# Modulation chunks issued as one run of eight products, and spread out over layer 0's feed-forward

## The chip, the cores and the metric

The kernel runs on one core of a Trainium2 chip. The metric is device microseconds (us) of one execution, the median of several runs.

## The reference

A transformer of two blocks on 256 tokens of width 1024, all in float32, inside tolerances that ask for nearly float32 products. The part that matters here is the first block: two layers, each with a modulation of six vectors for the tokens and six for a 256-token context, which are a small product with a large weight matrix.

```python
def adaln(cond, w_ada, b_ada):
    m = jax.nn.silu(cond) @ w_ada + b_ada
    return jnp.split(m, 6, axis=-1)
...
def first_block(x, c, ctx, c_ctx, w_ada, b_ada, g_mix, g_ffn, w_in, ...):
    for l in range(DEPTH):                      # DEPTH = 2
        sh1, sc1, gt1, sh2, sc2, gt2 = adaln(c, w_ada[l], b_ada[l])
        csh1, csc1, cgt1, csh2, csc2, cgt2 = adaln(c_ctx, w_ada[l], b_ada[l])
        h = rms_norm(x, g_mix[l]) * (1 + sc1) + sh1
        ...                                     # two attentions and a Fourier mix -> o
        x = x + gt1 * (o @ w_out[l])
        x = x + gt2 * swiglu(rms_norm(x, g_ffn[l]) * (1 + sc2) + sh2, w_gate[l], w_up[l], w_down[l])
        ...                                     # the context likewise, in layer 0 only
    return rms_norm(x, g_final)
```

`w_ada[l]` is 1024 x 6144 float32. The second block (two further layers with other attentions) has no modulation.

## The kernel before

Ordinary weights go in float32 through `raw` tiles of 128 x 2048 (1 MB). There are three of them (`raw_bufs`), filled in turn by loads that SyncE's queue issues in program order (L203). ScalarE casts each part of 1024 columns to its high half `whi` (L210), VectorE makes the low half `wlo` (L211), five of each exist, and every product of activations and weights is three matmuls: `mm3` at L336, L337 and L338. A load for a `raw` tile starts only when the tile's last reader is done.

The modulation of a layer is cut into twelve chunks (l, c) of 512 columns. `ada_chunk` (L469) takes two `raw` tiles from the same three, loads them (L483), and multiplies them without a cast: `ada_half` (L489) issues four products per tile, each with a stationary operand of 32 columns into its own 32 rows of one PSUM bank, so a chunk is eight products over two loads. The profile counts a float32 product of this kind twice, so a chunk shows as x16. `ada_columns` then copies the bank to `rows` on ScalarE (L496), transposes it in four pieces on TensorE (L498) and sums it on VectorE (L501, L502) into `mod`.

Layer 0's first four chunks have tiles of their own (`raw0`) and a fixed order. The other twenty go through `ada_chunk`: two a layer in the mixer (`ada_mid`), four a layer around the two groups of the first out-projection (`ada_att`, `out_first`), two in layer 1's `ada_gap` after the second part of the out-projection and the call that starts the feed-forward's norm (`norm_row`, `modulate`), and six, for the rest of layer 0 and the first of layer 1, in layer 0's feed-forward, at the groups that the table `ada_ffn` names (a group is two gate and two up columns with weights `w_gu`, 96 matmuls of 512 columns).

The program's order is not the engines' order. A scheduler with a model of the machine picks, for each engine, the ready instruction of best priority; `tc.cur_priority` moves work in that list, and the table `rank` holds the shifts. `together` (L316) gives its instructions a strong priority and ties the first of them to a list of instructions, here without a semaphore: the scheduler places it only once its model has those done. Each engine then runs its list strictly in that order.

Of the kernel before, what the change touches and what calls it, by code (L numbers as in the profile page):

```python
# [18 lines left out]
P = 128  # L19
# [3 lines left out]
RAW = 2048  # L23
# [232 lines left out]
class Build:  # L256
# [12 lines left out]
    ada_mid = ((0, 4), (0, 5)), ((1, 4), (1, 5))  # L269
    ada_att = ((0, 6), 0, (0, 7), (0, 9), 1, (0, 8)), ((1, 6), (1, 7), 0, 1, (1, 9), (1, 8))  # L270
    ada_gap = (), ((1, 10), (1, 11))
    ada_ffn = {3: ((0, 11), (0, 10)), 4: ((1, 0),), 8: ((1, 1),), 10: ((1, 3), (1, 2))}, {}

    rank = {"weights": 100, "weigh": -200, "qk": -200, "rope": -300, "hd2": -300, "together": 3000}

    def __init__(self, ctx, tc, d, out):
        self.tc, self.nc, self.d, self.out = tc, tc.nc, d, out
# [190 lines left out]

    def ada_chunk(self, l, c, tag="mm"):  # L469

        raws = self.ada_load(l, c, self.wp, "raw", self.raw_bufs)
        ps = self.bank(tag)
        for i in range(2):
            self.ada_half(ps, raws, i)
        self.ada_columns(l, c, ps, self.b1, 1)

    def ada_load(self, l, c, pool, tag, bufs):

        raws = []
        for i in range(2):  # L480
            off = (l * 12 + c) * P * 4096 + i * P * RAW
            raws.append(pool.tile([P, RAW], F32, tag=tag, name=tag, bufs=bufs))
            self.nc.sync.dma_start(raws[i], self.d["w_ada"][off:off + P * RAW].rearrange("(p f) -> p f", p=P))  # L483
        return raws

    def ada_half(self, ps, raws, i):

        for g in range(4):
            self.link(self.nc.tensor.matmul(ps[32 * g:32 * g + 32, :], self.s32[:, 4 * i + g, :], raws[i][:, 512 * g:512 * g + 512],  # L489
                                            start=i == 0, stop=i == 1))  # L490

    def ada_columns(self, l, c, ps, pool, bufs):

# [235 lines left out]
    def block1(self, ctx):  # L729
# [32 lines left out]
        self.nt_bufs = 8  # L762
        for s in (1, 0):
            nc.sync.dma_start(self.xs[s].rearrange("p a b -> p (a b)"), d["xT"][:, s * 2048:(s + 1) * 2048])
        load = lambda c: self.ada_load(0, c, self.np, "raw0", 4)
        first = {2: load(2), 0: load(0)}
        w_first = [WRows(self, d["w_in"], 0, 512, 2)]
        first[3], first[1] = load(3), load(1)
# [22 lines left out]
        for l in range(2):  # L791
# [5 lines left out]
            if l == 0:  # L797

                ps = [self.bank(tag) for tag in self.half_tags]
                for a in range(4):  # L800
# [4 lines left out]
                    for j, t in enumerate((2, 3, 0, 1)):  # L805
                        for k in (2 * a, 2 * a + 1):
                            c = slice(t * P, (t + 1) * P)
                            self.mm3(ps[j], [x[:, c] for x in h[k]], w_first[a // 2].get(k % 4), k == 0, k == KT - 1)
                        if (a, j) in ((0, 0), (0, 2)):
                            c = 3 - j  # L810
# [9 lines left out]
            else:  # L820
# [4 lines left out]
                ps = None  # L825
# [14 lines left out]
            with tc.tile_pool(name=f"ffn{l}", bufs=1, reuse_waits="tile") as fp:  # L840
# [15 lines left out]
                for gi, g in enumerate(FF_GROUPS):  # L856
                    acts = []
                    for f in range(f0, f0 + g, 2):
# [3 lines left out]
                        ps = [self.bank(tag) for tag in ("mm", "g") * 2]  # L862
# [22 lines left out]
                    for st in (apart if gi == 2 else [both]):  # L885
                        off = dn
                        for c in range(2):
                            ch = WCols(self, d["w_dn"], off, g, 4)
                            off = ch.off
# [384 lines left out]
```

## Time and profile before

| | |
|---|---|
| median of 3 runs | 1578.97 us (1578.86 to 1579.57) |
| the profiled execution | 1576.57 us |
| its span, first to last instruction | 1574.8 us |
| granted TensorE clock, mean | 0.992 |
| TensorE matmuls busy | 96% of the span |
| VectorE, ScalarE, GpSimdE busy | 64%, 51%, 4% |
| instructions | 25056 |

The span leaves out 1.8 us of the profiled execution's own time. Busy time says how long an engine had an instruction in it, not that the instruction was at the engine's best rate; what ended a wait is inferred from semaphores. The stages in the trace: layer 0's start and mixer up to about 232 us, its out-projection and norms to about 255 us, its feed-forward to about 650 us, layer 1's mixer and out-projection to about 787 us, layer 1's norm and feed-forward after that, and the second block from about 975 us.

### The profile page before, as it was taken

Reading aid. Unit: us, or ns where it says so; the run is one execution under the profiler, and the core shown is the slowest. Engines: PE = TensorE matmul, PEld = TensorE weight load, DVE = VectorE, ACT = ScalarE, POOL = GpSimd, SP = SyncE. Lnnn points to the kernel's source line nnn. Section 1 sums busy time; section 2 is a strip of 40 time slices with the busy share of each in tenths; the row PEclk is TensorE's granted clock in tenths of the full one; section 3 lists DMA queues with packets and bytes.
Section 4 is the critical chain, followed back from the end, with each engine's and each line's share of the span. In section 5 each row is a group of like instructions: output and inputs, shape, how many; then the busy total and the mean of one; then the engine's idle time right before and its main releaser. Section 6 shows DMA issues by size and latency. Waiting matters only on the chain.

```text
span 1574.8 us, 25056 instructions
## 1 busy us (share of the span) xinstructions
PE 1515.4 (96%) x9826; PEld 1293.9 (82%) x9826; DVE 1006.1 (64%) x2210; ACT 800.9 (51%) x1499; POOL 68.5 (4%) x83
## 2 busy tenths in 40 slices
PE   5999999999999999999989999999999999999997
PEld 2775679868788768865779999898999999899997
DVE  4674778233333325876565556998867779986775
ACT  3466756131222224557454445667764456776542
POOL 0200010000000000010000000102100000201000
PEclk9999999999999999999999999999999999999999
DMA  9311374252423334435565554434344544334451
GB/s 372 115 54 63 122 259 139 77 214 84 157 81 107 134 127 146 158 121 194 201 245 185 186 188 156 163 134 155 123 152 161 185 152 153 129 124 163 150 178 49
DMA packets 36982, 238.36 MB, mean 151 GB/s; under 512 B 4224, under 2 KB 5888, under 8 KB 15104
## 3 DMA queue, kind: packets, MB, share of 16 engines
q1 hardware_dynamic: 36576, 236.14, 42.4%
q8 instruction: 77, 1.26, 0.3%
q0 software_dynamic: 288, 0.62, 0.2%
q14 instruction: 41, 0.34, 0.1%
HBM read 236.32 MB, written 1.05 MB: 151 GB/s over the span
## 4 chain that ended last, share of the span: by engine, by line
PE 84%; DVE 9%; ACT 3%; issue 2%; DMA 1%; POOL 0%; SPq 0%; DVEq 0%; ACTq 0%; POOLq 0%
PE mm L336 11%; PE mm L338 11%; PE mm L337 10%; PE g L336 6%; PE g L337 6%; PE g L338 6%; PE dn L337 5%; PE dn L338 5%; PE dn L336 5%; PE mm L489 3%; DVE wlo L211 3%; PE tr L625 2%; PE pv L633 2%; PE pv L989 1%; PE mx L336 1%
## 5 line engine op out<-in xcount | busy, mean ns | idle before, releaser
L210 ACT CAST whi<-raw 128x1024 fp32r<-128x1024 f32 (+4 forms) x392 | 369.0, 948 | 452.8 <-PE mm L337 123.8
L211 DVE TENSOR_TENSOR wlo<-raw,whi 128x1024 fp32r<-128x1024 f32 (+4 forms) x392 | 430.5, 1105 | 177.8 <-ACT whi L210 175.4
L337 PE MATMUL dn<-Hl,whi 128*128 128x256 f32 (+1 forms) x520 | 161.2, 310 | 0.0
L336 PE MATMUL dn<-Hh,whi 128*128 128x256 f32 (+1 forms) x520 | 160.9, 310 | 0.1
L338 PE MATMUL dn<-Hh,wlo 128*128 128x256 f32 (+1 forms) x520 | 160.4, 309 | 0.4 <-DVE wlo L211 0.4
L338 PE MATMUL mm<-Hh,wlo 128*128 128x256 f32 (+1 forms) x512 | 149.4, 292 | 0.0
L337 PE MATMUL mm<-Hl,whi 128*128 128x256 f32 (+1 forms) x512 | 149.1, 291 | 0.0
L336 PE MATMUL mm<-Hh,whi 128*128 128x256 f32 (+1 forms) x512 | 149.0, 291 | 0.0
L336 PE MATMUL mm<-whi,Hh 128*128 128x384 f32 (+2 forms) x352 | 129.2, 367 | 0.0
L336 PE MATMUL mm<-Fh,whi 128*128 128x256 f32 (+1 forms) x368 | 123.8, 337 | 4.6 <-ACT whi L210 4.3
L338 PE MATMUL mm<-whi,Hl 128*128 128x384 f32 (+2 forms) x352 | 127.4, 362 | 0.0
L337 PE MATMUL mm<-wlo,Hh 128*128 128x384 f32 (+2 forms) x352 | 127.0, 361 | 0.0
L338 PE MATMUL mm<-Fh,wlo 128*128 128x256 f32 (+1 forms) x368 | 123.4, 335 | 1.2 <-DVE wlo L211 1.2
L337 PE MATMUL mm<-Fl,whi 128*128 128x256 f32 (+1 forms) x368 | 123.2, 335 | 0.0
L336 PE MATMUL g<-Fh,whi 128*128 128x256 f32 (+1 forms) x368 | 122.3, 332 | 0.4 <-ACT whi L210 0.4
L338 PE MATMUL g<-Fh,wlo 128*128 128x256 f32 (+1 forms) x368 | 122.0, 332 | 0.3 <-DVE wlo L211 0.3
L337 PE MATMUL g<-Fl,whi 128*128 128x256 f32 (+1 forms) x368 | 122.1, 332 | 0.0
L336 PEld LDWEIGHTS dn<-Hh,whi 128*128 128x128 f32 x520 | 99.0, 191 | 6.5 <-issue 0.8
L337 PEld LDWEIGHTS dn<-Hl,whi 128*128 128x128 f32 x520 | 99.2, 191 | 5.7 <-DVE Hl L878 0.7
L338 PEld LDWEIGHTS dn<-Hh,wlo 128*128 128x128 f32 x520 | 99.0, 191 | 5.6 <-DVE wlo L211 0.6
L336 PEld LDWEIGHTS mm<-Hh,whi 128*128 128x128 f32 x512 | 97.8, 191 | 1.2 <-issue 0.4
L337 PEld LDWEIGHTS mm<-Hl,whi 128*128 128x128 f32 x512 | 97.8, 191 | 1.1 <-issue 0.3
(284 smaller groups left out, 3252.3 us busy)
## 6 DMA issues: line engine op xcount, KB each, us to landing
raw<-in_w_ada_dram SPq DMA_DIRECT2D x48, 1024.0 KB, 5.0
raw<-in_w_gu_dram SPq DMA_DIRECT2D x44, 1024.0 KB, 4.9
raw<-in_w_mix_dram SPq DMA_DIRECT2D x32, 1024.0 KB, 4.8
raw<-in_w_in_dram SPq DMA_DIRECT2D x40, 768.0 KB, 4.3
raw<-in_w_in_dram SPq DMA_DIRECT2D x20, 1024.0 KB, 4.8
raw<-in_w_dn_dram SPq DMA_DIRECT2D x16, 1024.0 KB, 4.8
raw<-in_w_dn_dram SPq DMA_DIRECT2D x12, 768.0 KB, 4.4
raw<-in_w_out_dram SPq DMA_DIRECT2D x8, 1024.0 KB, 4.8
```

Of the source, the lines that this page charges most:

```text
L210: nc.scalar.copy(hi[:, :m], x)
L211: nc.vector.tensor_tensor(lo[:, :m], x, hi[:, :m].bitcast(F32), op=ALU.subtract)
L336: self.link(nc.tensor.matmul(out, lhs[0], rhs[0], start=start, stop=False))
L337: self.link(nc.tensor.matmul(out, lhs[0], rhs[1], start=False, stop=False))
L338: self.link(nc.tensor.matmul(out, lhs[1], rhs[0], start=False, stop=stop))
L489: self.link(self.nc.tensor.matmul(ps[32 * g:32 * g + 32, :], self.s32[:, 4 * i + g, :], raws[i][:, 512 * g:512 * g + 512], start=i == 0, s ...
L625: nc.tensor.transpose(ps[:, (2 * j + qt) * P:(2 * j + qt + 1) * P], p[i][:, qt, c:c + P], self.ident)
L633: first(nc.tensor.matmul(pv[i * 64:i * 64 + 64, :256], v, pts[i][0][:, j * 256:j * 256 + 256], start=b == 0 and j == 0, stop=b == nk // 2 ...
L989: f(nc.tensor.matmul(pv[64 * i:64 * i + 64, c], vs[i][j], pt[:, d], start=first and j == 0, stop=last and j == 1))
```

## The change

`ada_load` also returns its two load instructions. `ada_chunk` issues all eight products inside `together(loads)`, in the order second tile, first tile, so the scheduler places them as one run and only where its model has both loads done; and `ada_columns` is put in at a lower priority (`rows`, -60), so copy and transposes come later than they did. The table `ada_ffn` puts its six chunks at six groups, none beside another. The startup's chunks keep their order (only the returned pair is unpacked). No load, product or transpose is added or removed.

```diff
-    ada_ffn = {3: ((0, 11), (0, 10)), 4: ((1, 0),), 8: ((1, 1),), 10: ((1, 3), (1, 2))}, {}
+    ada_ffn = {1: ((0, 11),), 2: ((0, 10),), 4: ((1, 0),), 6: ((1, 1),), 8: ((1, 3),), 9: ((1, 2),)}, {}
-    rank = {"weights": 100, "weigh": -200, "qk": -200, "rope": -300, "hd2": -300, "together": 3000}
+    rank = {"weights": 100, "weigh": -200, "qk": -200, "rope": -300, "hd2": -300, "rows": -60, "together": 3000}
...
-        raws = self.ada_load(l, c, self.wp, "raw", self.raw_bufs)
+        raws, loads = self.ada_load(l, c, self.wp, "raw", self.raw_bufs)
         ps = self.bank(tag)
-        for i in range(2):
-            self.ada_half(ps, raws, i)
+        with self.together(loads) as add:
+            for i in (1, 0):
+                for ins in self.ada_half(ps, raws, i, 1):
+                    add(ins)
+        self.tc.cur_priority -= self.rank["rows"]
         self.ada_columns(l, c, ps, self.b1, 1)
+        self.tc.cur_priority += self.rank["rows"]
...
-    def ada_half(self, ps, raws, i):
+    def ada_half(self, ps, raws, i, first=0):
+        made = []
         for g in range(4):
-            self.link(self.nc.tensor.matmul(ps[32 * g:32 * g + 32, :], self.s32[:, 4 * i + g, :], raws[i][:, 512 * g:512 * g + 512],
-                                            start=i == 0, stop=i == 1))
+            made.append(self.nc.tensor.matmul(ps[32 * g:32 * g + 32, :], self.s32[:, 4 * i + g, :], raws[i][:, 512 * g:512 * g + 512],
+                                              start=i == first, stop=i != first))
+            self.link(made[-1])
+        return made
```

The change moves lines: L483, L489, L498 of before are L487, L494, L505 after it, and L590, L625 are L597, L632.

**SyncE's queue, layer 0's feed-forward.** Before, from the first load of gate and up weights on (gu are the gate and up weights, dn the down weights, ada the modulation's):

```order
L203 DMA raw<-in_w_gu_dram 128x2048 x6
L483 DMA raw<-in_w_ada_dram 128x2048 x4
L203 DMA raw<-in_w_gu_dram 128x2048 x2
L203 DMA raw<-in_w_dn_dram 128x2048 x4
L483 DMA raw<-in_w_ada_dram 128x2048 x2
L203 DMA raw<-in_w_gu_dram 128x2048 x8
```

The same stretch after the change:

```order
L203 DMA raw<-in_w_gu_dram 128x2048 x2
L487 DMA raw<-in_w_ada_dram 128x2048 x2
L203 DMA raw<-in_w_gu_dram 128x2048 x2
L487 DMA raw<-in_w_ada_dram 128x2048 x2
L203 DMA raw<-in_w_gu_dram 128x2048 x4
L203 DMA raw<-in_w_dn_dram 128x2048 x4
```

Four chunk loads in a row, for three tiles, became two pairs with two weight loads between them; the second place, near the stage's end, changes in the same way.

**TensorE, layer 1's attention.** Before, a stretch of the four chunks' products (L489) between transposes (tr, L625), scores (sc, L590 and L591) and turned rows (L498):

```order
L489 MATMUL mm<-raw,s_83 32x512 x3
L625 MATMUL tr<-ident,p 128x128
L489 MATMUL mm<-raw,s_83 32x512
L625 MATMUL tr<-ident,p 128x128 x3
L590 MATMUL sc<-kt,qt 128x512
L591 MATMUL sc<-kt,qt 128x512
L498 MATMUL mm<-ident,rows 128x128 x4
L489 MATMUL mm<-raw,s_83 32x512
L625 MATMUL tr<-ident,p 128x128 x4
```

After it, the end of the stretch from the second chunk's run to the third's (ahead of these rows, since the second run, stand six scores and two transposes):

```order
L597 MATMUL sc<-kt,qt 128x512
L598 MATMUL sc<-kt,qt 128x512
L505 MATMUL mm<-ident,rows 128x128 x2
L597 MATMUL sc<-kt,qt 128x512
L598 MATMUL sc<-kt,qt 128x512
L505 MATMUL mm<-ident,rows 128x128 x2
L597 MATMUL sc<-kt,qt 128x512
L598 MATMUL sc<-kt,qt 128x512
L597 MATMUL sc<-kt,qt 128x512
L598 MATMUL sc<-kt,qt 128x512
L632 MATMUL tr<-ident,p 128x128
L494 MATMUL mm<-raw,s_83 32x512 x8
```

A chunk's products stood in pieces of one to four, and are now eight together; so are all eight chunks of layer 1, and four of the six in layer 0's mixer and first out-projection, where the other two are cut into one and seven.

**VectorE, layer 1's norm ahead of the feed-forward.** Before, the reciprocal root (rn, L346 to L350) runs with two small steps of a chunk in it:

```order
L346 TENSOR_SCALAR rn<-rn 128x2
L348 TENSOR_TENSOR rn_t<-rn 128x2
L349 SCALAR_TENSOR_TENSOR rn_t<-rn_t,ms 128x2
L350 SCALAR_TENSOR_TENSOR rn<-rn_t,rn 128x2
L348 TENSOR_TENSOR rn_t<-rn 128x2
```

After the change, the same steps (their lines do not move):

```order
L346 TENSOR_SCALAR rn<-rn 128x2
L211 TENSOR_TENSOR wlo<-raw,whi 128x1024
L348 TENSOR_TENSOR rn_t<-rn 128x2
L211 TENSOR_TENSOR wlo<-raw,whi 128x1024
L349 SCALAR_TENSOR_TENSOR rn_t<-rn_t,ms 128x2
L350 SCALAR_TENSOR_TENSOR rn<-rn_t,rn 128x2
L348 TENSOR_TENSOR rn_t<-rn 128x2
```

Three low halves of weights (a third stands a few rows further on) are inside the chain, and two just ahead of it; before, none was. On TensorE the two `ada_gap` runs went from between the norm's steps to places 49 and 10 rows ahead of the norm's first step, among the last out-projection products, with 38 such products between the two runs. From layer 1's feed-forward on, all engines have the same order as before.

## Rows read from the trace of the kernel before

**Rows 1.** Page, part 1: busy us, share of the span, instructions, by engine.
```profile
PE 1515.4 (96%) x9826; PEld 1293.9 (82%) x9826; DVE 1006.1 (64%) x2210; ACT 800.9 (51%) x1499; POOL 68.5 (4%) x83
```
**Rows 2.** Timeline of SyncE's queue, 270 to 325: start, us, what, count.
```profile
274.45 44.79 SPq L483 DMA_DIRECT2D raw<-in_w_ada_dram  x4
```
**Rows 3.** Timeline of PE, 317.4 to 328.9, wait before it in brackets.
```profile
317.47 0.39 PE L338 MATMUL g<-Fh,wlo 128*128 128x512 f32 x1
317.79 2.76 PE L489 MATMUL dn<-raw,s 128*32 128x512 f32 x18
...
323.69 1.06 PE L489 MATMUL dn<-raw,s 128*32 128x512 f32 x8 [1.56 <-DMA raw<-in_w_ada_dram]
...
327.23 0.50 PE L336 MATMUL mm<-Fh,whi 128*128 128x512 f32 x1 [1.06 <-ACT whi L210]
```
**Rows 4.** Chain that ended last, around 320 and 580: start, us, what.
```profile
319.77 6.34 DMA raw<-in_w_gu_dram
...
580.14 6.38 DMA raw<-in_w_gu_dram
```
**Rows 5.** Timeline of PE: first products of stretches in layer 0's feed-forward.
```profile
272.90 0.40 PE L336 MATMUL mm<-Fh,whi 128*128 128x512 f32 x1
...
351.65 0.40 PE L336 MATMUL dn<-Hh,whi 128*128 128x512 f32 x1
...
532.74 0.50 PE L336 MATMUL mm<-Fh,whi 128*128 128x512 f32 x1
...
610.62 0.28 PE L336 MATMUL dn<-Hh,whi 128*128 128x256 f32 x1
```
**Rows 6.** Timeline of PE around a chunk that stands alone.
```profile
394.95 0.39 PE L338 MATMUL dn<-Hh,wlo 128*128 128x512 f32 x1
395.27 1.92 PE L489 MATMUL dn<-raw,s 128*32 128x512 f32 x16
397.13 0.50 PE L336 MATMUL mm<-Fh,whi 128*128 128x512 f32 x1
...
399.53 0.39 PE L338 MATMUL mm<-Fh,wlo 128*128 128x512 f32 x1
```
**Rows 7.** Timeline of PE: products with transposes in two groups between them.
```profile
175.35 0.40 PE L338 MATMUL mm<-Hh,wlo 128*128 128x512 f32 x1
...
176.50 0.39 PE L338 MATMUL mm<-Hh,wlo 128*128 128x512 f32 x1
```
**Rows 8.** Windows, L489 on PE alone: window, length, busy (count), clock, DMA share, GB/s.
```profile
140.00:220.00 80.00, 16.52 (x96) 1.00 0.44 160
692.00:735.00 43.00, 13.51 (x64) 1.00 0.54 188
...
755.00:786.00 31.00, 5.30 (x32) 1.00 0.68 251
786.00:795.00 9.00, 5.09 (x32) 1.00 0.69 259
```
**Rows 9.** Chain that ended last, in layer 1's attention.
```profile
699.27 0.97 PE mm L489 x2
```
**Rows 10.** Page, part 6: loads, KB each, median us from issue to landing.
```profile
raw<-in_w_ada_dram SPq DMA_DIRECT2D x48, 1024.0 KB, 5.0
```
**Rows 11.** Chain that ended last, layer 1's norm ahead of the feed-forward.
```profile
786.77 0.12 PE dn L338
...
793.39 1.28 DVE nt L528 x3
...
799.12 1.14 DVE wlo L211
...
800.89 0.21 PE mm L336
```
**Rows 12.** Timeline of PE: the feed-forward's first products in layer 1.
```profile
798.58 0.39 PE L336 MATMUL mm<-Fh,whi 128*128 128x256 f32 x1 [2.13 <-ACT whi L210]
...
800.31 0.58 PE L338 MATMUL mm<-Fh,wlo 128*128 128x256 f32 x1 [1.23 <-DVE wlo L211]
```
**Rows 13.** Windows: length, busy of PE, PEld, DVE, ACT, POOL, clock, DMA share, GB/s.
```profile
800.00:802.00 2.00, 1.69 (x8) 1.69 (x9) 2.00 (x5) 2.00 (x3) 0.00 (x0) 0.50 0.07 29
```

More of the change, by code (lines that the diff above doesn't have):

```diff
@@ L469, in ada_chunk @@
     def ada_chunk(self, l, c, tag="mm"):
-        raws = self.ada_load(l, c, self.wp, "raw", self.raw_bufs)
+        raws, loads = self.ada_load(l, c, self.wp, "raw", self.raw_bufs)
         ps = self.bank(tag)
-        for i in range(2):
-            self.ada_half(ps, raws, i)
+        with self.together(loads) as add:
[3 more added lines that the diff above has]
+        self.tc.cur_priority -= self.rank["rows"]
         self.ada_columns(l, c, ps, self.b1, 1)
+        self.tc.cur_priority += self.rank["rows"]
     def ada_load(self, l, c, pool, tag, bufs):
-        raws = []
+        raws, loads = [], []
         for i in range(2):
@@ L482, in ada_load @@
             raws.append(pool.tile([P, RAW], F32, tag=tag, name=tag, bufs=bufs))
-            self.nc.sync.dma_start(raws[i], self.d["w_ada"][off:off + P * RAW].rearrange("(p f) -> p f", p=P))
-        return raws
-    def ada_half(self, ps, raws, i):
+            loads.append(self.nc.sync.dma_start(raws[i], self.d["w_ada"][off:off + P * RAW].rearrange("(p f) -> p f", p=P)))
+        return raws, loads
+    def ada_half(self, ps, raws, i, first=0):
+        made = []
         for g in range(4):
-            self.link(self.nc.tensor.matmul(ps[32 * g:32 * g + 32, :], self.s32[:, 4 * i + g, :], raws[i][:, 512 * g:512 * g + 512],
-                                            start=i == 0, stop=i == 1))
+            made.append(self.nc.tensor.matmul(ps[32 * g:32 * g + 32, :], self.s32[:, 4 * i + g, :], raws[i][:, 512 * g:512 * g + 512],
+                                              start=i == first, stop=i != first))
+            self.link(made[-1])
+        return made
     def ada_columns(self, l, c, ps, pool, bufs):
@@ L764, in block1 @@
             nc.sync.dma_start(self.xs[s].rearrange("p a b -> p (a b)"), d["xT"][:, s * 2048:(s + 1) * 2048])
-        load = lambda c: self.ada_load(0, c, self.np, "raw0", 4)
+        load = lambda c: self.ada_load(0, c, self.np, "raw0", 4)[0]
         first = {2: load(2), 0: load(0)}
```

## The prediction

> **What bounds the kernel now.** I read the page's busy shares first: TensorE has work for 96% of the span [rows 1], so only two things can shorten this kernel: TensorE's own idle time, and work on TensorE that takes longer than it needs. I then looked at where the modulation's products stand, on TensorE's timeline and in the chain that ended last, in three places.
>
> First, layer 0's feed-forward. Two chunks stand next to each other there, twice. Four loads for three tiles were issued one behind the other, and the last of them had to wait until TensorE had read the first chunk: the four issues take 44.79 us from 274.45, so the last one ended at 319.24 [rows 2], after the first chunk's products had begun at 317.79 [rows 3]. TensorE waits 1.56 us for it at 323.69. The next gate and up weights are behind it on SyncE's queue, so they land 6.34 us after 319.77 [rows 4], and the first product with them starts at 327.23, behind a cast [rows 3]. The reader is to see one chain there: tile taken, load late, weights later. The same is there at 580.14 [rows 4].
>
> Second, the attention stages. A product with a 32-column operand that stands alone takes 0.97 us (the profile counts it as x2) [rows 9], while eight in one run take 1.92 [rows 6]: four of them, for four groups of rows, go side by side. A chunk cut into pieces pays 0.97 for every piece.
>
> Third, layer 1's norm. Two chunks run there inside the norm's chain (x32 between 786 and 795 [rows 8]), while TensorE has little else to do, and the feed-forward's first product comes 5.2 us after the first modulated part at 793.39 [rows 11, 12].
>
> **Feed-forward of layer 0.** One matmul of 512 columns in a dense stretch takes (317.47 - 272.90) / 191 = 0.2333 us [rows 3, 5]. From 272.90 to 351.65 there are three groups, 288 matmuls, or 67.2 us; the stretch took 78.75 [rows 5], so the pair and its stall cost 11.55. From 532.74 to 610.62 it is 77.88 - 67.2, less 0.45 for four transposes of an earlier chunk: 10.2. Together 21.75.
>
> Afterwards these are four chunks that stand alone. One that already did cost 399.53 - 394.95 - 9 x 0.2333 = 2.5 us with its transposes and no stall [rows 6]. The lower priority puts the transposes apart, between single matmuls. Four transposes in two groups cost 1.15 - 3 x 0.233 = 0.45 [rows 7], 0.22 a group, so four groups cost 0.9 in place of 0.45: 2.9 a chunk. Gain: 21.75 - 4 x 2.9 - 2 x 0.45 for the two chunks that already stood alone = 9.25. The loads should be hidden: two weight loads, with a group of 22.4 us (96 x 0.2333) of products, lie between one chunk's loads and the next one's. The bounds: 11.75 if transposes stay together, 6.1 if two runs still wait 1.56 each.
>
> **Attention of layer 0.** Six chunks have 16.52 us of busy time [rows 8]. Four in one run of 1.92, and two cut into one and seven, which have to pass three times (one, three, four) at 0.97: 7.7 + 5.8 = 13.5. Gain 3.0, less 0.7 for transposes standing apart. One wait is new: the products read the second tile first, so the first tile, which the next chunk's second load needs, is free only when the run ends; that load then takes 0.33 to issue and 5.0 to land [rows 10], 5.3 in all. Between the second and third run stand transposes, four weighted sums and Fourier products, some 4.5 us: a wait of 0.8. Net 1.5, between -2 (no gain from the pieces' order, and a wait of 1.56 as in rows 3) and +4.
>
> **Attention and out-projection of layer 1.** Four chunks go from 13.51 to 7.7, two more from 5.30 to 3.8 [rows 8]: 7.3. Waits by the same reckoning: between the second and third run stand fourteen scores (0.23 each) and seven transposes (0.12), 4.1 us, so 1.2 of 5.3 is left over; the fourth comes 4.5 us after the third (0.8) and the sixth 3.6 after the fifth (1.7). Together 3.7. TensorE reaches the end of the out-projection 3.6 us earlier.
>
> A rule of the Trainium skill would make this term another. Rows 6 show what entering a run costs: 395.27 - 394.95 is 0.32 for a matmul of 0.233, about 0.1 us, against the 0.97 of a lone product. The page "TensorEngine Tiling (Array Packing)", Key Properties, says that a change of the tiling mode drains TensorE. If that drain were all that a piece costs, the four chunks, now in 11 pieces and then in 4, would gain some 7 x 0.2 = 1.4 in place of 5.8, by this an estimate; the trace speaks for the larger figure, since the time sits in the products.
>
> **Layer 1's norm gives it back.** The two gap runs now stand among the last out-projection products: 2 x 1.92 = 3.8 on TensorE's path. The second follows the first by 38 products of 0.12 [rows 11], 4.6 us, so it waits 0.8 for its load; the first stands behind out-projection weights for its tiles, which I take at 1.4 (between nothing and 5.3). VectorE's chain for the norm has one low half between its sum and its first step and three inside, at 1.14 each [rows 11]: 4.5 later, and more if those weights' loads are late. Against this, the feed-forward's weights are then cast. The trace names 2.13 and 1.23 of waits for them [rows 12], and the whole wait from the first modulated part is 5.2: I take 4.3. So -3.8 - 2.2 - 4.5 + 4.3 = -6.2, and layer 1 as a whole 3.6 - 6.2 = -2.6, between -8 and +5. Behind this nothing moves: the order of every engine is the same from there on.
>
> **Sum:** 9.25 + 1.5 - 2.6 = 8.2 us. The profiled execution took 1576.57, so 1568.4; it lay 2.4 below the median shown, so 1570.7, in round numbers **1570.5**. About 0.2%, or 3.2 us, is what a measurement of this kernel tells from no change: faster means below 1575.8, slower above 1582.1.
>
> **Rivals.**
>
> *Layer 1 keeps its lead.* If VectorE reaches the norm with those low halves done (they only delay what is not yet due), the 4.5 falls away and so does the 1.4: +5.9, the sum 14.1, the time 1564.8. For it: VectorE is busy 64% of the span [rows 1]. Against: TensorE gets there sooner than now, and the weights' loads wait for the gap chunks' tiles.
>
> *The clock stays low over the first feed-forward products.* After the norm's thin stretch the granted clock is 0.50 [rows 13], the lower of the two levels (1.2 of 2.4 GHz), a 256-column matmul takes 0.21 instead of 0.12 [rows 11], and about 26 of them do so. The first group has 96: if all ran so, 70 x 0.093 = 6.5 us more, and 1577. The change takes sixteen products out of that stretch, so TensorE has less to do ahead of it than now. The page "TensorE: Matmul & The Clock Gate", Part 1, has it that the throttled level is the default and that activity lifts it; by this the stretch after a longer idle would be slower, as rows 13 have it after the present one.
>
> *Runs wait at the head of TensorE's queue (slower).* A run wants both loads, and the products behind it cannot pass. If the order on the chip runs ahead of the scheduler's model by a few us, each run waits, and everything behind it. The price is that of rows 3, 1.56 a wait: at fourteen of the twenty runs 21.8, less the 4.5 counted above, so 1570.7 + 17.3 = 1588. The change decides for slower from about 0.8 us a run beyond what I counted (11.4 / 14). For it: the three tiles are shared with weights whose casts wait for TensorE. Against: a chunk standing alone waited for nothing at 395.27 [rows 6]. The page on TensorE named above, Part 3, says that matmuls keep strict order, which is the rule that speaks against this change; rows 3 agree, where nothing passed the late product.
>
> *The feed-forward's stall only moves.* If each of the six single chunks makes the weights behind it late by 1.6 us, the 9.25 is used up: 1580, no change. For it: the two loads still go ahead of weights on one queue. Against: the product behind the run at 397.13 did not wait [rows 6].
>
> **How the numbers follow.** Forecast 0.60, with its own range of 1563 to 1576 from the bounds above; layer 1 keeps its lead 0.13; low clock 0.10; runs wait 0.09; stall moves 0.08. Faster: 0.57 + 0.13 + 0.04 = 0.74. Within 0.2%: 0.03 of the forecast, 0.06 of the low clock, 0.07 of the moved stall, 0.16. Slower: 0.09 + 0.01 of the moved stall = 0.10. The range from 1561 to 1579 holds the forecast, most of the first two rivals and part of the last: 8 in 10.
>
> **What would show it.** Right: no wait for a modulation load and no low clock near 320 and 580; the stretches of 288 matmuls with their chunk some 70 us long; the chunks' products with three passes less in layer 0's attention and 7.7 us for four chunks in layer 1's. The layer 1 term is wrong if the first feed-forward product there does not come about 6 us later, relative to the last out-projection product, than without those runs. The prediction is wrong if waits for modulation loads on TensorE add up to more than about 10 us, or if weights come late behind each single chunk.

## The result, and the profile after

The changed kernel took 1558.46 us (median of 4 runs, 1557.46 to 1559.08), against 1578.91 for the kernel before beside it: ratio 0.9871, interval 0.9854 to 0.9888, or 20.5 us faster. The forecast was 8.4 faster with a range that ended at 1561. The direction was right, the size was not.

The profiled execution took 1557.46 with a span of 1555.7. Its page, part 1:

```profile
PE 1498.9 (96%) x9826; PEld 1291.0 (83%) x9826; DVE 1003.9 (65%) x2210; ACT 800.9 (51%) x1499; POOL 67.2 (4%) x83
```

TensorE is busy 16.5 us less with the same 9826 matmuls [rows 1], and the span is 19.1 shorter: most of the gain is time in which instructions held TensorE, and the rest was idle time.

To see where, the program is cut at five matmuls that both kernels have, read from TensorE's timeline: the feed-forward's first product in layer 0, the first projection of layer 1, the last product of layer 1's out-projection, the first product of its feed-forward, and its first down product. The lengths, in us:

| | up to layer 0's feed-forward | feed-forward | layer 1, mixer and out-projection | norm | first gate and up groups |
|---|---|---|---|---|---|
| before | 246.13 | 400.33 | 140.15 | 11.97 | 49.50 |
| after | 241.97 | 388.25 | 140.07 | 11.52 | 46.97 |
| difference | -4.2 | -12.1 | -0.1 | -0.5 | -2.5 |
| forecast | -1.5 | -9.25 | +2.4 | +0.2 for both | |

(The forecast's +2.4 is the 3.6 gained in the attention less 6.0 for the two runs and their waits; its +0.2 is 4.5 less 4.3.) From there to the end of the span it is 726.7 before and 726.9 after.

**Layer 0's feed-forward.** SyncE's queue, 253 to 300:

```profile
254.52 0.33 SPq L203 DMA_DIRECT2D raw<-in_w_gu_dram  x1
255.38 11.73 SPq L487 DMA_DIRECT2D raw<-in_w_ada_dram  x2
271.59 9.03 SPq L203 DMA_DIRECT2D raw<-in_w_gu_dram  x4
```

The two modulation loads in this stretch are out within 11.73 us, where four took 44.79 [rows 2], and the weights follow. TensorE over the whole feed-forward, first before and then after; last, the kernel before behind its first stall (length, busy, granted clock, DMA):

```profile
246.13:646.46 400.33, 392.44 (x1973) 1.00 0.36 127
...
241.97:630.22 388.25, 387.76 (x1974) 1.00 0.37 131
...
328.00:331.20 3.20, 3.02 (x7) 0.50 1.01 348
```

Idle time fell from 7.9 to 0.5, which is 7.4 of the 12.1. The chunks' products alone (L489, L494) went from 13.62 to 11.54, since none is in pieces any more: 2.1. After the first stall the granted clock was 0.50, the lower level, for eight products at 0.43 in place of 0.233: 1.6, and after the change the clock does not fall in this stage. About 1 us is left without a name.

On TensorE's timeline the second chunk and, ten us on, its transposes:

```profile
271.44 0.40 PE L338 MATMUL mm<-Fh,wlo 128*128 128x512 f32 x1
271.77 1.93 PE L494 MATMUL dn<-raw,s 128*32 128x512 f32 x16
273.62 0.50 PE L336 MATMUL mm<-Fh,whi 128*128 128x512 f32 x1
...
274.19 0.40 PE L338 MATMUL mm<-Fh,wlo 128*128 128x512 f32 x1
...
282.36 0.40 PE L337 MATMUL g<-Fl,whi 128*128 128x512 f32 x1
282.59 0.27 PE L505 MATMUL dn<-ident,rows 128*128 128x128 f32 x1
282.62 0.48 PE L338 MATMUL g<-Fh,wlo 128*128 128x512 f32 x1
...
283.97 0.39 PE L336 MATMUL mm<-Fh,whi 128*128 128x512 f32 x1
```

No wait stands behind the run. The run costs 274.19 - 271.44 - 3 x 0.233 = 2.05 (three products start in that time), and the four transposes between five products 283.97 - 282.36 - 5 x 0.233 = 0.44: 2.5 a chunk, as before [rows 6], where they stood together. So transposes that stand apart cost no more.

**Attention.** L494 on TensorE alone, in windows that hold the same chunks as in rows 8:

```profile
110.00:215.00 105.00, 13.62 (x96) 1.00 0.34 128
...
670.00:710.00 40.00, 7.69 (x64) 1.00 0.60 214
735.00:755.00 20.00, 3.85 (x32) 1.00 0.58 212
755.00:775.00 20.00, 3.85 (x32) 0.99 0.93 359
```

16.52 became 13.62 and 13.51 became 7.69, as forecast to a tenth. The waits for the runs' loads did not come as forecast. Layer 1's, from TensorE's timeline:

```profile
686.11 1.92 PE L494 MATMUL mm<-raw,s 128*32 128x512 f32 x16 [0.28 <-DVE mod L508]
693.01 1.92 PE L494 MATMUL mm<-raw,s 128*32 128x512 f32 x16
700.59 1.92 PE L494 MATMUL mm<-raw,s 128*32 128x512 f32 x16 [1.11 <-DMA raw<-in_w_ada_dram]
740.55 1.92 PE L494 MATMUL mm<-raw,s 128*32 128x512 f32 x16
...
760.91 1.92 PE L494 MATMUL mm<-raw,s 128*32 128x512 f32 x16 [0.36 <-DMA raw<-in_w_ada_dram]
767.51 1.92 PE L494 MATMUL mm<-raw,s 128*32 128x512 f32 x16
```

0.28 + 1.11 + 0.36 = 1.75, in place of the 5.9 counted, and the first of these is not for a load. The runs that are not shown did not wait for one. A premise of the count failed too: it lets the next chunk's second load go out when a run ends. On SyncE's queue the loads behind the third, fifth and seventh run (693.01, 740.55, 760.91) are:

```profile
694.14 0.33 SPq L487 DMA_DIRECT2D raw<-in_w_ada_dram  x1
...
741.67 0.33 SPq L487 DMA_DIRECT2D raw<-in_w_ada_dram  x1
...
762.03 0.33 SPq L487 DMA_DIRECT2D raw<-in_w_ada_dram  x1
```

Each goes out 1.1 us after its run's start, 0.8 before the run's end; why the tile is free by then is not shown. The sixth run started at 746.72, 4.25 after the fifth ended, and did not wait, where the forecast had 1.7.

**Layer 1's norm.** TensorE from the last out-projection product to the feed-forward at the full clock:

```profile
770.29 0.28 PE L338 MATMUL dn<-Hh,wlo 128*128 128x256 f32 x1
...
779.63 0.66 PE L369 MATMUL tr<-ident,rn 128*128 128x128 f32 x2 [5.56 <-DVE rn L350]
781.81 0.58 PE L336 MATMUL mm<-Fh,whi 128*128 128x256 f32 x1 [1.52 <-ACT Fh L536]
...
785.12 0.28 PE L338 MATMUL g<-Fh,wlo 128*128 128x256 f32 x1
```

VectorE's first modulated part (L528 before):

```profile
780.73 1.27 DVE L535 SCALAR_TENSOR_TENSOR nt<-xs,gain,acc 128x256 f32<-128x256 f32 x3 [1.25 <-ACT acc L523]
```

The wait of 5.56 for the root is in the main the three low halves inside VectorE's chain; without them it is 2.48 (low halves behind the root, below). With the chunks gone from this gap TensorE idles 9.0 us in it, against 4.7. The first modulated part was started 6.5 us after the last product's end before (793.39 against 786.89 [rows 11]), and 10.2 after it now (780.73 against 770.57): 3.7 later, 4.5 forecast. But the products no longer wait for weights [rows 12]: the first comes 1.1 after that part instead of 5.2, no wait for a low half follows (1.23 before), and the full clock is back 3.3 us after the first product, not 7.2.

That last difference is not a shorter low clock. Windows of TensorE, the first two of before, the others of after (length, busy, granted clock, DMA):

```profile
799.10:805.70 6.60, 5.39 (x25) 0.50 0.49 171
805.90:810.00 4.10, 4.10 (x37) 1.00 0.76 312
...
770.00:774.60 4.60, 2.11 (x17) 1.00 0.90 381
774.80:781.80 7.00, 0.66 (x2) 0.50 0.90 318
781.80:785.00 3.20, 3.19 (x15) 0.50 0.00 0
785.10:790.00 4.90, 4.90 (x44) 1.00 0.01 3
```

The lower level lasted 10.2 us, against 6.6 before, but 7.0 of them lay ahead of the first product, where TensorE had 0.66 us of work. So fewer products ran at it, some 14 in place of some 26. The table's 2.5 for the first groups is the wait of 1.23 and, for the rest, these products.

### The profile page after: what moved, and what is told of

The parts are those of the page before. It is cut to its first block, busy times and chain, and to the rows that moved or that the text cites. A ratio compares the mean times of both kernels' runs of the same rounds, so it can differ in the third digit from the quotient of the medians.

```text
span 1555.7 us, 25050 instructions
## 1 busy us (share of the span) xinstructions
PE 1498.9 (96%) x9826; PEld 1291.0 (83%) x9826; DVE 1003.9 (65%) x2210; ACT 800.9 (51%) x1499; POOL 67.2 (4%) x83
## 3 DMA queue, kind: packets, MB, share of 16 engines
HBM read 236.32 MB, written 1.05 MB: 153 GB/s over the span
## 4 chain that ended last, share of the span: by engine, by line
PE 82%; DVE 10%; ACT 3%; DMA 2%; issue 2%; POOL 0%; SPq 0%; ACTq 0%; POOLq 0%; DVEq 0%
PE mm L336 11%; PE mm L337 10%; PE mm L338 10%; PE g L337 6%; PE g L336 6%; PE g L338 6%; PE dn L337 5%; PE dn L338 5%; PE dn L336 5%; DVE wlo L211 3%; PE mm L494 2%; PE tr L632 2%; PE pv L640 2%; PE pv L996 1%; PE mx L336 1%
## 5 line engine op out<-in xcount | busy, mean ns | idle before, releaser
L338 PEld LDWEIGHTS mm<-Hh,wlo 128*128 128x128 f32 x512 | 97.9, 191 | 1.6 <-issue 0.8
```

What stands on the lines that cost most here:

```text
L338: self.link(nc.tensor.matmul(out, lhs[1], rhs[0], start=False, stop=stop))
```

## The experiments

Theory S, after the result: three parts in three stages. The table takes the two stalls away (12), the runs take pieces out of the attentions (4 in layer 0, 5 ahead of layer 1's out-projection), and moving the gap chunks costs about what it returns. The rivals are named with each run. Every run is measured against the kernel before on the same chip; the stage lengths are read as in the table above, each from one profiled execution. Many of the intervals overlap, so the stages carry the argument: up to the feed-forward the five kernels with rows at -60 and runs held for both loads take 241.55 to 242.67, the five with rows at 0 237.38 to 238.56, and the feed-forward of the five kernels with the new table, six chunks there and runs held for both loads takes 388.08 to 388.25. The first gate and up groups scatter more, with the clock, as the gap experiment shows.

**The table alone**, the kernel before with the new `ada_ffn`:

```diff
-    ada_ffn = {3: ((0, 11), (0, 10)), 4: ((1, 0),), 8: ((1, 1),), 10: ((1, 3), (1, 2))}, {}
+    ada_ffn = {1: ((0, 11),), 2: ((0, 10),), 4: ((1, 0),), 6: ((1, 1),), 8: ((1, 3),), 9: ((1, 2),)}, {}
```

> The kernel before with the new table alone: no two chunks next to each other in layer 0's feed-forward, products and rows in the old order. Theory S (the parts add up): the two stalls go with the table, 12.1 us less in the feed-forward as in the changed kernel, nothing elsewhere: 1578.9 - 12.1 = 1566.8, within 1.5. Rival R (the run is needed there too, since a chunk in pieces takes its tiles longer): half of it or less, 1573 or more.

1567.67 (ratio 0.9936, 0.9922 to 0.9950). The feed-forward took 390.41, 9.9 less. So the table alone is enough for most of it, with products and rows in the old order.

**The run alone**, the changed kernel with the old table (the diff above, the other way round).

> The changed kernel with the old table: two pairs next to each other again, each in one run held for both loads. Theory S: layer 0 up to its feed-forward 4.2 faster than before, layer 1 3.0 faster, the pairs' stalls as before: 1578.9 - 7.2 = 1571.7, within 1.5. Rival R: a run held for both loads waits longer beside another chunk, since its second load needs the first chunk's tile: over 1574. Third: the run alone takes the stalls away: near 1560.

1559.06 (0.9881, 0.9868 to 0.9895): the third case. The feed-forward took 388.74, 11.6 less, with two pairs of neighbours in the program. SyncE's queue, and the two runs on TensorE:

```profile
271.01 13.93 SPq L487 DMA_DIRECT2D raw<-in_w_ada_dram  x4
290.61 3.21 SPq L203 DMA_DIRECT2D raw<-in_w_gu_dram  x2
```

```profile
282.62 1.92 PE L494 MATMUL dn<-raw,s 128*32 128x512 f32 x16
...
292.37 1.92 PE L494 MATMUL dn<-raw,s 128*32 128x512 f32 x16
```

The same four loads, 13.93 us instead of 44.79 [rows 2]. The runs have `together`'s priority, so the scheduler takes a run as soon as its model has the loads, puts 7.8 us of other products between the two, and frees the tiles. In the kernel before, the load for the first chunk's second tile went out at 280.86:

```profile
280.86 0.33 SPq L483 DMA_DIRECT2D raw<-in_w_ada_dram  x1
```

By the 5.0 to landing of rows 10 the chunk was there at about 286, and its products came at 317.79 [rows 3], some 32 us later; here the first run comes 5.2 after the issue of its second load (277.43). The stall came from tiles held by products that could have gone, and neighbours only made it show. Theory S falls here: the two parts are two cures for the same 12 us.

**Halves, each held for its own load**, first half first:

```diff
-        with self.together(loads) as add:
-            for i in (1, 0):
-                for ins in self.ada_half(ps, raws, i, 1):
+        for i in (0, 1):
+            with self.together(loads[i:i + 1]) as add:
+                for ins in self.ada_half(ps, raws, i, 0):
                     add(ins)
```

> The changed kernel with each half of a chunk, four products, held for its own load alone, first half first. Theory E (the strong priority is what counts, not that both loads are there): the feed-forward as in the changed kernel but some 0.3 us a chunk for a second entry, no stall; the attentions up to 3 slower through pieces: 1559 to 1563. Theory H (the hold for both loads is what counts): the tiles are held between the halves and the stalls come back, 1567 or more.

1561.32 (0.9894, 0.9877 to 0.9910), as theory E (early) has it: the feed-forward 389.53, 1.3 over the changed kernel for four chunks that are entered twice, and no stall beyond one wait of 0.44 for a load. With the new table, then, the hold for both loads is not needed in the feed-forward. But that table has no such stall without any run either (390.41 above), so this does not tell the early start from the hold where chunks are neighbours: halves with the old table were not tried.

**Rows at the old priority**, so copy and transposes are no longer put back by 60:

```diff
-    rank = {"weights": 100, "weigh": -200, "qk": -200, "rope": -300, "hd2": -300, "rows": -60, "together": 3000}
+    rank = {"weights": 100, "weigh": -200, "qk": -200, "rope": -300, "hd2": -300, "rows": 0, "together": 3000}
```

> The changed kernel with the priority of copy and transposes back to that of the products (rank rows 0). Theory S: a transpose costs 0.11 us on TensorE whether it stands alone or not, and the wait for the copy was seldom on the path: within 2 of the changed kernel, 1557 to 1560.5. Rival P (the step of the prediction, transposes apart cost 0.45 a chunk more): 2.7 faster for six chunks, 1556, down to 1550 for twenty. Rival W (transposes close behind the run make TensorE wait for ScalarE's copy, 0.7 each): up to 14 slower.

1554.12 (0.9851, 0.9838 to 0.9865): by the medians 4 faster than the changed kernel, by the spans of the profiled executions 3.0, with intervals that overlap; and not where rival P said: the feed-forward took 388.08, the same as with rows apart. The gain is before it, 237.75 against 241.97; 1.3 of it is lost again at the norm and the first groups (12.08 and 47.75). The changed kernel in layer 0's attention:

```profile
156.28 0.47 PE L336 MATMUL mm<-Hh,whi 128*128 128x512 f32 x1 [0.69 <-DVE mod L508]
...
176.41 1.05 PE L494 MATMUL mm<-raw,s 128*32 128x512 f32 x2
177.39 1.08 PE L640 MATMUL pv<-pt,v 128*64 128x256 f32 x8
178.40 1.92 PE L494 MATMUL mm<-raw,s 128*32 128x512 f32 x14
```

A product waits for a chunk's sum on VectorE (L508), the last reader of its PSUM bank: the tag `mm` has two, and late rows hold one of them longer. And two runs are cut into one and seven. With rows at priority 0 all six chunks are whole, L494 alone in the same window:

```profile
110.00:215.00 105.00, 11.54 (x96) 1.00 0.38 141
```

That is 2.1 less; waits on TensorE over 0.1 us between 100 us and the feed-forward fall from 1.9 in all to 0.1. Of the 1.9 only the 0.69 is named as a wait at a bank; the others are for steps of the attention, and why late rows make those, or cut two runs, is not shown. The lower priority, which the forecast priced at 0.45 a chunk in the feed-forward, costs nothing there and 4.2 here.

**The gap chunks in halves, as before the change:**

```diff
                     for a in self.ada_gap[l]:
-                        self.ada_chunk(*a)
+                        self.ada_chunk(*a, halves=1)
```

(with `halves` the four and four products are issued by `ada_half` without `together`, and the rows at the old priority).

> The changed kernel with the two gap chunks of layer 1 issued as before (two halves, no run), so that they stand inside the norm's gap again. Theory S: what they cost among the out-projection's products (4.3) they gave back through weights that were ready: from the last out-projection product to the feed-forward at full rate 19.1 before, 19.6 now with the runs counted in: within 1.5 of the changed kernel, 1557 to 1560. Rival P (the step of the prediction: the move gives back 6.2): some 5 us faster, 1553.5.

1556.13 (0.9860, 0.9847 to 0.9874), which overlaps with the changed kernel's interval. The stages tell more: mixer and out-projection 134.76 against 140.07, norm 11.97 against 11.52, the first groups 48.31 against 46.97. So the move costs 5.3 on the way and returns 1.8: 3.5 net in this pair, and 4.3 with rows at 0 (the kernels of the runs on rows and on rows and gap together). Theory S (nothing) is wrong and the forecast's step (6.2) is too large. The returned part is not firm: the chunks stand in the gap again in both, yet the first groups take 48.31 here and 49.51 with rows at 0, and the clock is at 0.50 for 3.3 us here and for 6.7 there. What sets that is not shown. TensorE's timeline shows the old waits back:

```profile
776.45 0.39 PE L336 MATMUL mm<-Fh,whi 128*128 128x256 f32 x1 [2.12 <-ACT whi L210]
...
778.19 0.58 PE L338 MATMUL mm<-Fh,wlo 128*128 128x256 f32 x1 [1.23 <-DVE wlo L211]
```

**Low halves behind the root's last step**, order only:

```diff
-                nc.vector.tensor_tensor(lo[:, :m], x, hi[:, :m].bitcast(F32), op=ALU.subtract)
+                low = nc.vector.tensor_tensor(lo[:, :m], x, hi[:, :m].bitcast(F32), op=ALU.subtract)
+                if b.hold:
+                    if b.hold.pop(0):
+                        b.tc.add_manual_dep(getattr(low, "ins", low), getattr(b.last_rn, "ins", b.last_rn).name, NOSYNC, reason="after the norm")
...
-            nc.vector.scalar_tensor_tensor(y, t, 1.5, y, op0=ALU.add, op1=ALU.mult)
+            self.last_rn = nc.vector.scalar_tensor_tensor(y, t, 1.5, y, op0=ALU.add, op1=ALU.mult)
...
+                self.hold = [0, 0, 1, 1, 1] if l == 1 else []
```

(The list is for the first five parts of layer 1's gate and up weights.)

> The changed kernel, with three low halves of weights tied behind the last step of layer 1's norm on VectorE (the order alone, no semaphore), so that none stands inside the chain. Theory S: the spread on TensorE comes 3.4 earlier (three times 1.14), but two of the low halves are then needed before they are made, which takes 1 to 3 back: 0.5 to 2.5 faster than the changed kernel. Rival: VectorE's order there does not matter, since the weights' casts set the feed-forward's start: within 0.5.

1555.33 (0.9851, 0.9838 to 0.9864). The norm took 8.74 against 11.52, and the groups behind it 46.90 against 46.97: 2.8 faster, nothing given back, a little more than theory S had. TensorE's waits there:

```profile
776.37 0.66 PE L373 MATMUL tr<-ident,rn 128*128 128x128 f32 x2 [2.48 <-DVE rn L354]
778.84 0.58 PE L340 MATMUL mm<-Fh,whi 128*128 128x256 f32 x1 [1.81 <-ACT Fh L540]
```

The wait for the root is 2.48 in place of 5.56, three low halves less.

**Gap chunks moved to layer 0's feed-forward:**

```diff
-    ada_gap = (), ((1, 10), (1, 11))
-    ada_ffn = {1: ((0, 11),), 2: ((0, 10),), 4: ((1, 0),), 6: ((1, 1),), 8: ((1, 3),), 9: ((1, 2),)}, {}
+    ada_gap = (), ()
+    ada_ffn = {1: ((0, 11),), 2: ((0, 10),), 3: ((1, 0),), 5: ((1, 1),), 6: ((1, 3),), 7: ((1, 2),), 8: ((1, 10),), 9: ((1, 11),)}, {}
```

> The changed kernel with layer 1's two gap chunks moved into layer 0's feed-forward (eight chunks at eight groups there, none in the gap). Theory S: two more chunks at 2.5 us each there, 4.7 less among the out-projection's products of layer 1, the norm behind it as in the changed kernel: within 1.5 of it, 1557 to 1560. Rival N (with no chunk's loads before it, the feed-forward's weights come so early that VectorE is through with them before the norm): 3 to 4 faster, 1555.

1556.50 (0.9869, 0.9848 to 0.9889), by its ratio not told apart from the changed kernel. The feed-forward took 5.0 more for two chunks (393.23), the mixer and out-projection 4.7 less (135.34), as reckoned; the norm was 8.52, 3.0 shorter, since VectorE was through with all five low halves before the root's first step: rival N's mechanism. By the stages it is 2.4 faster, which the runs do not confirm.

**Rows and gap together** (both diffs above), then **the same with the old table**, then **one chunk moved** ((1, 10) to the feed-forward, (1, 11) left in the gap in halves) and **both moved**, all with rows at priority 0.

> Rows at the products' priority and the gap chunks as before, in halves. Theory S: the two add up, since they act in different stages: 4.7 in layer 0's mixer and 3.4 in layer 1's gap off the changed kernel's 1558.5: 1550.5, within 1.5. Rival: the gap stays at what the kernel before loses there and swallows any lead: 1554.

1551.31 (0.9833, 0.9818 to 0.9848): they add up, 6.8 in the span against 3.0 and 3.5 singly.

> The kernel of the run before this one with the old table, so two pairs of chunks next to each other again. Theory E (products that go ahead as soon as their loads are there free the tiles, so neighbours do not matter): within 1 of that run. Theory T (the table takes the stalls away): 12 slower.

1552.70 (0.9841, 0.9826 to 0.9855), feed-forward 388.77 against 388.10. Theory E again: without the table the feed-forward loses 0.7 of the 12. Whether the table is worth a microsecond beside the run stays open, since the intervals overlap.

> Rows at the products' priority, chunk (1,10) moved to layer 0's feed-forward, (1,11) alone left in the gap, in halves. Theory S: 2.7 more in the feed-forward, the gap half as long in loads, so the feed-forward's weights come in time: 2 to 4 less there than with two chunks in it: 1550, between 1549 and 1552. Rival: the run goes ahead of the gap as one among the out-projection's products and costs 2.2 there: 1553.

1550.23 (0.9820, 0.9807 to 0.9833). As theory S has it: the feed-forward took 2.45 more than with rows and gap together (390.55 against 388.10), and norm and first groups 2.7 less (9.63 + 49.14 against 11.97 + 49.51), so it gains nothing over that kernel. The chunk's eight products stand right behind the last out-projection product, not among them.

> Rows at the products' priority and both gap chunks moved to layer 0's feed-forward. Theory S: what these two did singly adds up: 4.8 in layer 0's mixer, 5.5 given in the feed-forward, 6.2 taken in the gap where the changed kernel gave back 1.5: 1558.5 - 4.8 + 5.5 - 4.7 - 3 = 1551.5, between 1550 and 1553. Rival: the lead is lost again at layer 1's attention: 1555.

1550.64 (0.9822, 0.9809 to 0.9835): norm 8.50, feed-forward 393.11, the two single effects together.

The last two and the kernel with rows and gap together beat both kernels, by 26 to 29 us against the one before; among the three nothing is told apart.

## Why the prediction was wrong in size

Most of its mechanisms were there, and its sign was right; four terms of the sum were mis-sized, each by 2.5 to 3.2 us and all the same way, the first two beyond their own bounds (11.75 and 4).

- *Feed-forward, 9.25 forecast, 12.1 measured.* The step that failed is "the lower priority puts the transposes apart ... 0.9 in place of 0.45". Rows 7 are two groups of transposes between three products; I took half of the 0.45 as a price for each group, and it is a price for four transposes, 0.11 each, however they stand: four apart measured 0.44. With 2.5 a chunk the same sum gives 11.75, which was the upper bound; 0.3 more came. The attribution failed as well: I gave the stall to neighbours in the table, and the run alone takes it away too.
- *Layer 0's attention, 1.5 forecast, 4.2 measured.* The 3.0 of busy time came as worked out (2.9). The 0.8 of waiting and the 0.7 for transposes did not come, and TensorE idled 1.1 less than before in this stage (3.1 to 2.0 between 100 us and the feed-forward). What I did not see at all is that the priority of the rows costs 4.2 there: 2.1 in pieces and 1.8 in waits, 0.69 of them at a PSUM bank. The stage could have given 8.4.
- *Layer 1's mixer and out-projection, 2.4 slower forecast, 0.1 faster measured.* Busy time as worked out (7.3). The step that failed is the waits, 3.7 and 2.2 in the sum: for loads 1.5 were measured, not 5.9. The load that a run frees goes out 0.8 before the run's end, not behind it, and the products between two runs are not dense: two waits elsewhere, 0.58 and 0.35, cover a late load too. The two runs among the out-projection's products cost 4.2 with their entries, 3.8 in the sum, and new short waits took part of the gain back.
- *Norm and first groups, 0.2 slower forecast, 3.0 faster measured.* The later norm was right (3.7 against 4.5). What ready weights are worth was 4.3 in the sum and 5.3 in the trace: 4.1 up to the first product and 1.2 for the low half. Another 1.3 are products no longer at the lower clock, which the sum left out; that is luck, since the clock had fallen early enough to spend most of its low time idle. By the prediction's own sign, a first product about 6 us later, this term is wrong: it came 0.5 sooner.

Of the rivals, "layer 1 keeps its lead" came nearest, but by another way: the norm was as late as forecast. The low clock did come, 0.50 again, and for longer, 10.2 us against 6.6, with the sixteen products gone from the thin stretch; its price did not, since 7.0 of the 10.2 lay ahead of the first product and the full level was back 3.3 after it and not 7.2. Runs hardly waited at the queue's head: 1.5 us in two waits outside the start, against 21.8 priced. The stall did not move on: no wait follows the run at 271.77.

The drain that the Trainium skill's page "TensorEngine Tiling (Array Packing)", Key Properties, speaks of can be no more than about 0.1 us at each border of a run in these rows (2.05 for a run whose products take 1.85). The products in pieces cost the rest, as the fall from 13.51 to 7.69 shows.

## What to carry to other kernels

Where transfers share a few buffers, ask not only what is loaded next to what, but how long a filled buffer waits for its reader: work that could run at once and stands late in an in-order queue stalls every load behind it. A few small instructions that free a buffer or a bank should go first (the chunks' products here by priority; their rows too, which cost 4.2 in one stage when they were put back and gained nothing in another), and a chain that other engines wait for should have no bulk work placed inside it. Price a small instruction by itself before pricing how it is spread. And where the clock falls in a thin stretch, look at when it falls as well as for how long: low time in which the engine idles costs little.

## What was not expected of the hardware

Seven products of 32 columns in a row (x14) took 1.92 us, as long as eight (x16), and one alone 1.05, in the rows above; in the kernel before one, three and four by themselves took 1.05, 1.06 and 1.07. So the price here is by passes of up to four, each about 0.95, and a pass that is not full costs the same. Eight such products split one and seven therefore cost three passes.
